# A hybrid decoder on one core: the PSUM bank of mLSTM's value sums

## The chip, the core and the metric

The kernel runs on one NeuronCore of a Trainium2 chip, as one launch. The metric is device time in microseconds (us) from start to end of an execution, the median of the executions taken. The engines are called PE (TensorE), ACT (ScalarE), DVE (VectorE), POOL (GpSimd) and SP (SyncE, which issues most DMAs). PSUM, where PE's results land, has eight banks.

## The reference

Two decoder layers work on 512 tokens of width 1024 in float32. Each layer projects the normalised input to four mixers of 256 columns each, sums their outputs through `w_out`, then adds cross attention on 256 memory rows and a gated feed-forward network. The four mixers are hgrn2 (a gated recurrence in chunks), DSA (an index branch picks 128 keys for each query, then attention on those), NSA (compressed, selected and window attention) and mLSTM. What matters here is mLSTM, head by head, and the two others that use the bank in question:

```python
# mLSTM, one chunk of one head
s   = einsum('td,sd->ts', q, k) * d_mat          # scores times decay
num = ... + einsum('ts,sv->tv', s, v)            # value sums
den = ... + sum(s, axis=-1)
h   = num / max(abs(den), exp(-m_t))
# DSA, index branch
rel   = relu(einsum('thd,sd->hts', iq, ik))
score = einsum('hts,th->ts', rel, iw);  idx = top_k(score, 128)
# NSA
o = gate0 * o_cmp + gate1 * o_slc + gate2 * o_swa
```

The kernel takes mLSTM over all 512 tokens at once instead of in chunks, and takes its denominators from a 65th column of ones beside the 64 value columns.

## The kernel before, in words

Matrix products keep float32 accuracy by splitting each operand into a high and a low part, so that most products are three matmuls (`mm_T`, lines 329 to 331 of the profile; `mm_tok`, lines 339 to 341). Weights come by DMA, are split by ACT and POOL (lines 292, 293), or come already split.

**Stages of a layer.** Stage one, inside the first `weave` of `run`, holds the input projections (`proj_T`, `proj_tok`), DSA's index branch and top-k (`dsa`), all of NSA (`nsa`, `nsa_cmp`) and all of mLSTM (`ml`). Stage two, the second `weave`, holds DSA's attention, hgrn2 (`hg`), the part of the output projection that needs NSA and mLSTM (`out_stage(0)`), the memory's keys and values (`xa_kv`) and `out_stage(1)`. Then come cross attention and the feed-forward network. In layer 0, stage one lies at about 25 to 273 us of the span and in layer 1 at about 850 to 1100 us.

**The order of work.** The parts are generators. `mix` always advances the one that is least far along, by the costs that they yield against totals in the table `COST`. That fixes one program order. The scheduler of the tile framework then takes program order as priority, sets every engine's own order by a simulated timeline, and puts in the waits. On the chip each engine runs its list in order.

**PSUM in stage one.** The tags and their banks: `acc` two (projections), `tp` one, `sc` two and `o` one (NSA's attention), `dt` one, `mb` one. A tag with one bank holds one tile at a time, and a tile gives up the bank when its last reader has run.

- `mb` is mLSTM's own: two row transposes (L493) and two column transposes (L992), then for each of four heads four score tiles (L1048; DVE multiplies each by the decay into `m_p0` to `m_p3`, L1056, which have one buffer each) and one tile of value sums (20 matmuls, L1065). DVE reads the sums twice: a copy of the denominators (L1069) and, after three small steps, the product into `mo` (a `tt` call, L351). The next head's first scores then get the bank.
- `dt` is shared by DSA's index branch (by the aliases of its pool: transposes of the queries L493 and, per block of queries, eight score tiles L679, each read by ACT at L681) and NSA's compressed branch (L1200, L1208, L1220, L1239, L1244, L1263). At NSA's end two tiles of it take the compressed values (L1161), each read by DVE into `mo`, which needs NSA's window and selected attention to be done.

Counting the yields of the generators gives the program order of the tiles on `dt`, in both layers: index block 1 (two transposes, eight scores); of index block 2 two transposes and one score; two tiles of the compressed branch (L1200, L1208); the other seven scores of block 2; the rest of the compressed branch up to L1263; block 3 (two transposes, eight scores); the two L1161 tiles. mLSTM's first score tile comes after all of these in program order, and then mLSTM's heads 0, 1, 2, 3, each with four score tiles and its sums. In time, mLSTM's heads run beside NSA's attention and index block 3.

mLSTM's convolutions for heads 2 and 3 (L1006 to L1016) write `m_hi0` and `m_hi1`, with one buffer each, which the scores of heads 0 and 1 read.

**Around the end of stage one.** The top-k of block 3 (`select`, L696 and L697) runs 16 rounds on DVE. The projection `hgi` writes `h_v` (L485), whose memory is that of the index branch. `out_stage(0)` transposes mLSTM's output (L1281 into `tp` of the second stage's banks) and multiplies it with `wo0` in eight groups on `acc`; behind these, on the same tag, come `xa_kv` and `out_stage(1)`.

Of the kernel before, what the change touches and what calls it, by code (L numbers as in the profile page):

```python
# [17 lines left out]
TB = S // 128  # L18
# [188 lines left out]
class Kernel:  # L207
# [760 lines left out]
    def ml(self, pool):  # L968
# [34 lines left out]
        def conv(c):  # L1003
            x = self.m_x[c]
            y = self.t2(pool, "m_y", [128, S])
            nc.scalar.activation(y, x[:, 0:S], AF.Identity, scale=self.col("conv_w", 4 * c), bias=self.col("conv_b", c))  # L1006
            for j in range(1, 4):
                nc.vector.scalar_tensor_tensor(y, x[:, j:j + S], self.col("conv_w", 4 * c + j), y, op0=OP.mult, op1=OP.add)
            th = self.t2(pool, "m_th", [128, S])
            nc.scalar.activation(th, y, AF.Tanh, scale=0.5)  # L1010
            z = th
            nc.vector.scalar_tensor_tensor(z, th, 1.0, y, op0=OP.add, op1=OP.mult)
            hi = self.t(pool, f"m_hi{c // 2}", [128, S], FR, bufs=1)
            lo = pool.tile([128, S], FR, name="m_lo", tag="m_x", bufs=4)
            nc.scalar.activation(hi, z, AF.Copy)
            self.tt(lo, z, hi.bitcast(FT), OP.subtract, nc.gpsimd)  # L1016
            return hi, lo
# [10 lines left out]
        for h in range(4):  # L1028
            po = 64 * (h % 2)
            if h % 2 == 0:  # L1030
                while h and self.m_have < 2:
                    yield 0.2
                q = conv(h // 2)
                yield 3.0
                k = conv(2 + h // 2)
                yield 3.0
            Mb = self.t(pool, "m_Mb", [128, S], bufs=2)
            nc.scalar.dma_start(Mb, bass.AP(tensor=dap.tensor, offset=dap.offset + h * S, ap=[[0, 128], [1, S]]))
            Md = self.t2(pool, "m_Md", [128, TB, 128])
            self.tt(Md, Mb.rearrange("p (t c) -> p t c", t=TB), self.k("mlm")[:, None, :].to_broadcast([128, TB, 128]),  # L1040
                    OP.add, nc.gpsimd)
            pT = []
            for sb in range(TB):
                n = S - sb * 128
                sc = self.psum("mb")
                r = slice(po, po + 64)
                for j, (kk, qq) in enumerate(((k[0], q[0]), (k[0], q[1]), (k[1], q[0]))):
                    nc.tensor.matmul(sc[:, :n], kk[r, sb * 128:sb * 128 + 128], qq[r, sb * 128:],  # L1048
                                     start=(j == 0), stop=(j == 2))
                d = self.t2(pool, "m_d", [128, S])  # L1050
                ac = a_col[:, sb, h:h + 1]
                nc.scalar.activation(d[:, 0:128], Md[:, sb], AF.Exp, bias=ac, scale=-1.0)
                if n > 128:
                    nc.scalar.activation(d[:, 128:n], Mb[:, sb * 128 + 128:], AF.Exp, bias=ac, scale=-1.0)
                p = self.t(pool, f"m_p{sb}", [128, n], bufs=1)
                nc.vector.scalar_tensor_tensor(p, sc[:, :n], 1.0 / 32, d[:, :n], op0=OP.mult, op1=OP.mult)  # L1056
                pT.append(p)
                yield 1.0
            while not self.m_have:
                yield 0.2  # L1060
            ps = self.psum("mb", (128, TB, 65))
            for tb in range(TB):
                for sb in range(tb + 1):
                    c = (tb - sb) * 128
                    nc.tensor.matmul(ps[:, tb], pT[sb][:, c:c + 128], self.m_v1[:, sb, h], start=(sb == 0), stop=(sb == tb))  # L1065
            hh = ho[:, :, h]
            den = self.t(pool, "m_den", [128, 4, TB])
            dc = ps[:, :, 64]
            nc.vector.tensor_copy(den[:, 0], dc)  # L1069
            nc.vector.scalar_tensor_tensor(den[:, 0], den[:, 0], -1.0, den[:, 0], op0=OP.mult, op1=OP.max)  # L1070
            self.tt(den[:, 0], den[:, 0], e_col[:, :, h], OP.max)
            nc.vector.reciprocal(den[:, 1], den[:, 0])
            self.tt(hh, ps[:, :, 0:64], den[:, 1, :, None].to_broadcast([128, TB, 64]), OP.mult)
            yield 1.0
            sq = self.t2(pool, "m_sq", [128, TB, 64])
            nc.scalar.activation(sq, hh, AF.Square)
            nc.vector.tensor_reduce(den[:, 2], sq, axis=AX.X, op=OP.add)
            self.rsqrt(pool, den[:, 3], den[:, 2], 4.0 / 64, 4 * EPS)
            self.tt(hh, hh, den[:, 3, :, None].to_broadcast([128, TB, 64]), OP.mult)
            self.tt(hh, hh, og4[:, :, h], OP.mult)  # L1080
            yield 1.0
# [549 lines left out]
```

## Time and profile before

| what | value |
|---|---|
| median of 3 runs | 1665.04 us (1662.25 to 1666.55) |
| the profiled execution's own time | 1668.55 us |
| its span | 1666.8 us |
| mean granted TensorE clock | 0.978 of full speed |
| PE busy | 1598.7 us, 96% of the span |
| DVE, ACT, POOL busy | 920.8, 711.5, 799.8 us |

The span goes from the first to the last instruction of the profiled execution; its time adds what lies around that. "Busy" is time in which the engine had an instruction in work, and the ends of pipelined matmuls are modelled. A granted clock of 1.00 is 2.4 GHz and 0.50 is 1.2 GHz.

### The profile page before, as it was taken

What the parts mean: (1) busy time and instruction counts of PE and PEld (TensorE: products, weight loads), DVE (VectorE), ACT (ScalarE), POOL (GpSimd) and SP (SyncE); (2) the same over time, 40 slices, a digit from 0 to 9 for tenths busy, and PEclk for the clock granted to TensorE, in tenths of its full rate; (3) what the DMA queues carried; (4) which work ended last, traced back from release to release, by engine and by line L of the source; (5) the groups of instructions that cost most, each with busy time, mean ns of one, the idle gap of its engine ahead of it and who ended that gap; (6) DMA issues with size and microseconds to landing.
All of it is one profiled execution on the core that took longest, in us unless ns stands there. A gap on an engine that the chain in (4) does not pass through costs nothing.

```text
span 1666.8 us, 25488 instructions
## 1 busy us (share of the span) xinstructions
PE 1598.7 (96%) x9262; PEld 1326.0 (80%) x9262; DVE 920.8 (55%) x1760; ACT 711.5 (43%) x1525; POOL 799.8 (48%) x698
## 2 busy tenths in 40 slices
PE   7899997999899989999999999999998999999999
PEld 7878876878788868888898887787877888888887
DVE  5697678976764330344225884779776544124420
ACT  5565453356654443343324443433665433223321
POOL 5664334566448987874412010145662444444442
PEclk9999997999999999999999999979999999999999
DMA  5342212213248999963355733131141233333331
GB/s 162 88 114 79 70 32 86 63 49 107 83 140 290 318 311 315 309 216 90 106 158 180 263 111 133 51 118 52 38 125 33 76 95 91 93 101 95 94 100 66
DMA packets 114365, 212.72 MB, mean 128 GB/s; under 512 B 12984, under 2 KB 30136, under 8 KB 114240
## 3 DMA queue, kind: packets, MB, share of 16 engines
q1 hardware_dynamic: 111888, 206.11, 39.8%
q10 hardware_dynamic: 2032, 3.94, 0.7%
q8 instruction: 73, 1.20, 0.3%
q0 software_dynamic: 320, 1.05, 0.2%
q14 instruction: 52, 0.43, 0.1%
HBM read 170.69 MB, written 40.35 MB: 127 GB/s over the span
## 4 chain that ended last, share of the span: by engine, by line
PE 82%; DVE 9%; issue 2%; DMA 2%; POOL 2%; ACT 2%; SPq 0%; ACTq 0%; POOLq 0%; DVEq 0%
PE acc L329 13%; PE acc L331 13%; PE acc L330 13%; PE sc L330 5%; PE sc L331 5%; PE sc L329 5%; PE acc L339 4%; PE acc L340 3%; PE acc L341 3%; PE hb L856 2%; PE o L574 2%; PE sc L552 2%; PE tp L493 2%; POOL wl L293 1%; PE mb L1048 1%
## 5 line engine op out<-in xcount | busy, mean ns | idle before, releaser
L293 POOL TENSOR_TENSOR wl<-wr,wh 128x512 fp32r<-128x512 f32 (+5 forms) x432 | 548.9, 1279 | 462.0 <-ACT wh L292 441.1
L292 ACT ACTIVATE wh<-wr 128x512 fp32r<-128x512 f32 (+5 forms) x432 | 252.4, 592 | 339.0 <-PE acc L330 137.1
L329 PE MATMUL acc<-xh,wh 128*128 128x512 f32 (+1 forms) x704 | 274.0, 391 | 1.6 <-DVE xT L466 0.7
L330 PE MATMUL acc<-xl,wh 128*128 128x512 f32 (+1 forms) x704 | 272.4, 387 | 0.0
L331 PE MATMUL acc<-xh,wl 128*128 128x512 f32 (+1 forms) x704 | 272.4, 387 | 0.0
L466 DVE TENSOR_TENSOR xT<-acc,xT 128x512 f32<-128x512 f32 (+1 forms) x112 | 67.8, 610 | 215.7 <-PE acc L331 215.5
L329 PEld LDWEIGHTS acc<-xh,wh 128*128 128x128 f32 x704 | 132.7, 189 | 32.5 <-issue 2.4
L331 PEld LDWEIGHTS acc<-xh,wl 128*128 128x128 f32 x704 | 132.5, 188 | 27.6 <-issue 0.4
L330 PEld LDWEIGHTS acc<-xl,wh 128*128 128x128 f32 x704 | 132.7, 189 | 26.4 <-issue 0.2
L329 PE MATMUL acc<-f_gh,wh 128*128 128x512 f32 x352 | 139.0, 397 | 6.7 <-ACT f_gh L1491 6.7
L339 PE MATMUL acc<-wh,xh 128*128 128x256 f32 (+2 forms) x480 | 140.1, 295 | 0.8 <-DMA wh<-whl 0.6
L330 PE MATMUL sc<-xl,wh 128*128 128x512 f32 x352 | 139.7, 397 | 0.0
L330 PE MATMUL acc<-f_gl,wh 128*128 128x512 f32 x352 | 139.3, 397 | 0.0
L331 PE MATMUL acc<-f_gh,wl 128*128 128x512 f32 x352 | 139.3, 397 | 0.0
L331 PE MATMUL sc<-xh,wl 128*128 128x512 f32 x352 | 138.8, 394 | 0.0
L340 PE MATMUL acc<-wl,xh 128*128 128x256 f32 (+2 forms) x480 | 138.4, 290 | 0.0
L329 PE MATMUL sc<-xh,wh 128*128 128x512 f32 x352 | 137.9, 393 | 0.0
L341 PE MATMUL acc<-wh,xl 128*128 128x256 f32 (+2 forms) x480 | 137.2, 288 | 0.0
L318 POOL TENSOR_TENSOR phl<-pr,phl 128x512 fp32r<-128x512 f32 (+3 forms) x72 | 94.7, 1316 | 37.4 <-ACT phl L317 30.9
L317 ACT ACTIVATE phl<-pr 128x512 fp32r<-128x512 f32 (+3 forms) x72 | 44.2, 613 | 137.6 <-DMA pr<-in_wst 127.8
L339 PEld LDWEIGHTS acc<-wh,xh 128*128 128x128 f32 x480 | 92.3, 193 | 5.1 <-issue 1.9
L340 PEld LDWEIGHTS acc<-wl,xh 128*128 128x128 f32 x480 | 92.8, 194 | 1.2 <-issue 0.5
(407 smaller groups left out, 3160.2 us busy)
## 6 DMA issues: line engine op xcount, KB each, us to landing
wr<-in_wst SPq DMA_DIRECT2D x332, 256.0 KB, 2.7
whl<-phl SPq DMA_DIRECT2D x52, 512.0 KB, 3.8
pr<-in_wst SPq DMA_DIRECT2D x52, 256.0 KB, 4.1
wh<-whl SPq DMA_DIRECT2D x52, 256.0 KB, 4.6
wl<-whl SPq DMA_DIRECT2D x52, 256.0 KB, 4.7
wr<-in_wst SPq DMA_DIRECT2D x48, 128.0 KB, 2.6
wr<-in_wst SPq DMA_DIRECT2D x32, 192.0 KB, 2.4
whl<-phl SPq DMA_DIRECT2D x8, 524.0 KB, 3.7
```

The costliest lines, as they stand in the source:

```text
L292: nc.scalar.activation(hi, raw, AF.Copy)
L293: nc.gpsimd.tensor_tensor(lo, raw, hi.bitcast(FT), op=OP.subtract)
L317: nc.scalar.activation(both[:, 0], raw, AF.Copy)
L318: nc.gpsimd.tensor_tensor(both[:, 1], raw, both[:, 0].bitcast(FT), op=OP.subtract)
L329: self.nc.tensor.matmul(acc, wh, xh, start=(j == 0), stop=False)
L330: self.nc.tensor.matmul(acc, wh, xl, start=False, stop=False)
L331: self.nc.tensor.matmul(acc, wl, xh, start=False, stop=(j == n - 1))
L339: self.nc.tensor.matmul(acc, xh[:, s], wh, start=(first and j == 0), stop=False)
L340: self.nc.tensor.matmul(acc, xh[:, s], wl, start=False, stop=False)
L341: self.nc.tensor.matmul(acc, xl[:, s], wh, start=False, stop=(last and j == n - 1))
L466: self.nc.vector.tensor_add(self.xT[c][:, cols], acc, self.xT[c][:, cols])
L493: self.nc.tensor.transpose(p[:rows, j * 128:j * 128 + 128], src(j), self.ident)
```

## The change

The tile of the value sums is asked for under the tag `dt` in place of `mb`; its shape, its matmuls and its readers stay as they are. The score tiles stay on `mb`. The number of banks stays as it is.

```diff
             while not self.m_have:
                 yield 0.2
-            ps = self.psum("mb", (128, TB, 65))
+            ps = self.psum("dt", (128, TB, 65))
             for tb in range(TB):
                 for sb in range(tb + 1):
```

## Rows read from the trace of the kernel before

**Rows 1.** The page: engines over the whole span, and the chain's shares by engine.
```profile
PE 1598.7 (96%) x9262; PEld 1326.0 (80%) x9262; DVE 920.8 (55%) x1760; ACT 711.5 (43%) x1525; POOL 799.8 (48%) x698
...
PE 82%; DVE 9%; issue 2%; DMA 2%; POOL 2%; ACT 2%; SPq 0%; ACTq 0%; POOLq 0%; DVEq 0%
```

**Rows 2.** Windows: stretch, length, busy us (instructions) per engine; granted clock, DMA share, GB/s.
```profile
178.00:240.00 62.00, 61.83 (x371) 47.77 (x370) 40.01 (x69) 32.92 (x73) 24.87 (x18) 1.00 0.23 64
240.00:273.00 33.00, 23.89 (x150) 17.46 (x150) 30.80 (x78) 9.16 (x24) 2.29 (x2) 0.77 0.26 84
273.00:300.00 27.00, 26.80 (x202) 25.47 (x200) 21.30 (x37) 12.81 (x27) 21.32 (x24) 0.90 0.21 58
300.00:345.00 45.00, 44.97 (x271) 35.53 (x272) 39.52 (x86) 15.36 (x42) 21.50 (x22) 1.00 0.18 51
...
1068.00:1096.00 28.00, 22.38 (x137) 17.13 (x136) 26.41 (x67) 8.35 (x20) 2.29 (x2) 0.78 0.26 88
```

**Rows 3.** Waits near stage one's end: PE and ACT, layer 0; PE and ACT, layer 1.
```profile
PE tp L1281 <- DVE mo L351: 4.1, 1, 4.1
...
ACT m_sq L1076 <- DVE mo L351: 13.0, 1, 13.0
...
PE mb L1048 <- DVE mo L351: 1.0, 1, 1.0
...
ACT m_sq L1076 <- DVE mo L351: 10.5, 2, 10.0
```

**Rows 4.** Timeline, layer 0: index block 2's operand, its scores, the compressed branch between.
```profile
83.27 0.57 ACT L497 ACTIVATE iqT<-dt 96x512 fp32r<-96x512 f32 x1
...
83.89 0.69 PE L679 MATMUL dt<-ikT,iqT 96*128 96x384 f32 x1 [2.08 <-ACT iqT L497]
...
103.14 0.34 PE L1200 MATMUL dt<-kc,n_hid 64*128 64x64 f32 x2
...
116.69 0.34 PE L679 MATMUL dt<-ikT,iqT 96*128 96x384 f32 x1
```

**Rows 5.** Timeline, DVE: the second L1161 tile read, layer 0 and layer 1.
```profile
260.68 0.69 DVE L351 TENSOR_TENSOR mo<-mo,dt 128x512 f32<-128x512 f32 x1
...
1086.61 0.68 DVE L351 TENSOR_TENSOR mo<-mo,dt 128x512 f32<-128x512 f32 x1
```

**Rows 6.** Timeline, layer 0: head 0's sums; head 3's first scores, sums and last read.
```profile
178.55 2.34 PE L1065 MATMUL mb<-m_v,m_p 128*128 128x65 f32 x20
...
254.45 0.49 PE L1048 MATMUL mb<-m_hi,m_hi 64*128 64x512 f32 x1
...
263.80 4.53 PE L1065 MATMUL mb<-m_v,m_p 128*128 128x65 f32 x20 [0.73 <-DVE m_p L1056]
...
271.90 0.41 DVE L351 TENSOR_TENSOR mo<-mb,m_den 128x256 f32<-128x256 f32 x1
```

**Rows 7.** Windows of one line: L1065 (two heads' sums), then L1048 (two heads' scores).
```profile
178.00:240.00 62.00, 4.91 (x40) 4.72 (x40) 1.00 0.23 64
...
990.00:1068.00 78.00, 6.17 (x24) 3.62 (x25) 1.00 0.29 99
```

**Rows 8.** Timeline, layer 0: `hgi`'s blocks leave `acc`, PE resumes; PE resumes in layer 1.
```profile
272.74 0.82 ACT L485 ACTIVATE h_v<-acc,r 128x256 f32<-128x256 f32 x2
...
273.25 0.58 PE L339 MATMUL acc<-wh,xh 128*128 128x256 f32 x1
...
1095.99 0.56 PE L339 MATMUL acc<-wh,xh 128*128 128x256 f32 x1
```

**Rows 9.** Timeline, layer 0: convolutions of heads 2 and 3, first and last step; second L1281.
```profile
218.41 0.74 DVE L1008 SCALAR_TENSOR_TENSOR m_y<-m_x,cols,m_y 128x512 f32<-128x512 f32 x1
...
231.66 0.63 ACT L1015 ACTIVATE m_hi<-m_th 128x512 fp32r<-128x512 f32 x1 [0.27 <-DVE m_th L1012]
...
302.78 0.60 PE L1281 MATMUL tp<-kc,mo 128*128 128x128 f32 x4
```

## The prediction

> **What bounds the kernel now.** The page first: PE is busy 1598.7 of 1666.8 us and 82% of the chain that ended last is PE, with DVE next at 9% [rows 1]. So all idle time of PE together is 68 us, and a change that adds no matmul can only move that idle time, or the clock. Then the windows around the place of the change, the second half of stage one and what follows [rows 2]. From 178 to 240 us PE is full (61.83 of 62.00). From 240 to 273 it is busy only 23.89 of 33.00 at a mean clock of 0.77, while DVE is busy 30.80: here DVE and the waits set the pace. From 273 on PE is full again (26.80 of 27.00, then 44.97 of 45.00). Layer 1 has the same hole (22.38 of 28.00 at 0.78). Third, the waits in that hole [rows 3]: PE stood 4.1 us before the first L1281, ACT 13.0 us before mLSTM's L1076, both for DVE's read of head 3's sums; in layer 1 ACT stood 10.5 us in two waits there, and PE 1.0 us for a score tile until the sums of the head before had been read. Last, the timeline of the tiles on `dt`, below.
>
> **What the change asks for.** On `mb` each head's first scores wait for the read of the sums before. With the sums on `dt` that wait goes. Its direct price is small: 1.0 us seen on PE in layer 1, and the L1281 wait of 4.1 us, which is a wait for the last read on a bank that the second stage takes over [rows 3]. No instruction is added or taken away.
>
> **Where the sums stand in the bank's row.** This decides the sum. The trace shows how `dt` is given out. Index block 2 had its transposed queries at 83.84 us (83.27 + 0.57) and its first score at 83.89; ACT read that at once, and yet the second score, with the same operands, came at 116.69. Between them lie the tiles of the compressed branch, which wasn't ready until 103.14 [rows 4]. The bank stood empty for some 18 us while a ready score waited: it goes round in program order, not to whoever is ready. Layer 1 repeats the pattern. mLSTM's sums come after the two L1161 tiles in program order. Those wait for NSA's end: the second was read by 261.37 us (260.68 + 0.69) in layer 0 and 1087.29 in layer 1 [rows 5]. Head 0's sums, at 178.55 now [rows 6], therefore start at about 261, or as much earlier as NSA ends earlier without mLSTM beside it (I allow up to 10 us). Heads 1 to 3 follow, since `m_p0` to `m_p3` have one buffer each and head 0's sums still have to read them. The scores of heads 1 to 3 keep `mb`, but only the first score of each head can be made ahead of its `m_p` buffer.
>
> The Trainium skill (PSUM — Partial Sum Buffer, Summary: rules for kernel authors) says that a bank that is read should not be the one that PE writes next, but a different one. By that rule the change is right, and it would save the waits just named and no more; the rows on `dt` speak against it here.
>
> **Term A, PE work that moves.** Two heads' sums take 4.91 us of PE and two heads' scores 6.17 at full clock [rows 7], so a head is 2.46 + 3.09 = 5.5 us. Now all four heads are done when PE becomes full again. After the change I expect head 0's sums and head 1's scores before that point, and head 1's sums and heads 2 and 3 behind it: 2.46 + 2 x 5.55 = 13.5 us of PE work. What they leave behind in 178 to 240 can't be filled: program order has no projection left that isn't held by `acc`, since `hgi`'s first two blocks sit in its two banks until 272.74 [rows 8]. Behind 273 PE is full, so the moved work adds its length. Bounds: 0 (all of it falls into later holes) and 22 us (four heads). Nearest rows: PE's windows behind 273, with 0.2 us idle in 72; I take 13.5.
>
> **Term B, an earlier restart.** PE resumed dense work at 273.25 and 1095.99 [rows 8], behind head 3's sums (263.80, 4.53 us at half clock) and, in layer 0, behind ACT's 13.0 us wait and PE's 4.1 us wait [rows 3, 6]. These orders go, since head 3 is then far behind. What stays is DVE's top-k, which fills DVE in that stretch (30.80 of 33.00 [rows 2]). Bounds of the gain: 0, and the 13.0 and 10.5 us that ACT stood. I take 6 us per layer: the 4.1 us wait plus some 2 us of mLSTM's DVE work that leaves the stretch.
>
> **Term C, behind it.** The chain of heads is now serial: from 261.4, head 0's sums 2.5, three heads of 13.9 (254.45 to 268.33 for head 3 [rows 6]), and the convolutions of heads 2 and 3, which wait for head 1's scores, 13.9 (218.41 to 232.29 [rows 9]); together 319 us, and some 4 us for the last read. The transposes of `mo` that `out_stage(0)` needs came at 302.78 [rows 9], so it may be 20 us late, or not at all if the heads run at PE's pace of 5.5 us. PE has hgrn2, DSA's attention and the moved 13.5 us to do meanwhile, which covers most of it. DVE was busy 39.52 of 45.00 from 300 on [rows 2], so hgrn2 gets a little later. Bounds 0 and 20 us; I take 3 us, nearer the lower end, because the moved work is the cover. If that cover fails, rival three is what is left.
>
> **Sum.** Per layer 13.5 - 6 + 3 = 10.5 us, for two layers 21 us. The profiled execution took 1668.55 us, 3.5 over the median of the runs, so the sum against its own time is 1689.6, and about 1686 beside the median.
>
> **The rivals.**
> *One, the bank goes to whoever is ready* (the change works as it reads). Head 0's sums at 178.55 would fall where `dt` is idle, and the later ones push the index scores by a few us at most. Gain: 4.1 + 1.0 us and about 1 us of small waits, 1659. Against it stand rows 4. Chance 0.10.
> *Two, the hole is filled.* The order holds, but with mLSTM out of the way ACT empties `hgi`'s blocks early and PE's projections run in the hole. Then B reaches its upper ends (23.5 us for both layers against 27 of A), and if PE keeps full clock there, a mean of 0.77 over 33 us and 0.78 over 28 us [rows 2] give back 7.6 + 6.2 us: 27 - 23.5 - 13.8 = -10, 1655. It decides once `h_v` leaves `acc` before about 262 us. Chance 0.12. Without the clock the two terms cancel to within 4 us: no change, 1668; chance 0.17.
> *Three, stage two starves.* The groups of `wo0` stand first on `acc`, and `xa_kv` and `out_stage(1)` queue behind them; if mLSTM ends near 323 instead of 272 us, PE has too little to do, and C is at its upper end: 13.5 - 6 + 20 = 27.5 per layer, 55 in all, 1720. It decides once mLSTM's last read is later than some 310 us in layer 0. Chance 0.20.
>
> **How the numbers follow.** My forecast has 0.41: 1686 us, by itself between 1673 and 1700. About 5 us (0.3%) is what a measurement of this kernel can tell from no change. Faster: 0.10 + 0.12 = 0.22. No change: 0.17. Slower: 0.41 + 0.20 = 0.61. The range runs from just under rival two's time to just under rival three's, 1653 to 1715; beyond it lie the far halves of these two, under 2 in 10.
>
> **What would show it.** Right: the first L1065 after the second read of an L1161 tile in both layers, four sets of sums close together behind some 255 us, `m_sq` no longer a 13 us wait of ACT, PE less than full before 240 and full at 265 to 300, and L1281 of mLSTM's output later than 302.78. The order of `dt` shows wrong if any L1065 stands before an index score of block 3. Term B is wrong if `h_v` still leaves at 272; term C if the next stage's PE windows show idle time of more than a few us. The forecast falls if the time is under 1670: then the moved work found a hole that I didn't see.

## The result, and the profile after

The changed kernel takes 1744.34 us (median of four runs, 1728.25 to 1762.37) beside 1665.8 us for the kernel before on the same chip: a ratio of 1.0435, 95% interval 1.0407 to 1.0464. It is slower by 78.5 us where the prediction said 21, and outside the range of 1653 to 1715. The ratio leaves out the slowest of the four executions, which counts as a slow one and is the one profiled, so that the trace shows a loss of 93.8 us of span (1760.6 against 1666.8).

The page of the changed kernel, engines over the span and the chain by engine:

```profile
PE 1667.0 (95%) x9257; PEld 1382.6 (79%) x9262; DVE 917.2 (52%) x1760; ACT 711.9 (40%) x1525; POOL 797.2 (45%) x698
...
PE 80%; DVE 10%; ACT 3%; issue 2%; DMA 2%; POOL 2%; SPq 0%; another core or an unknown queue 0%; ACTq 0%; POOLq 0%; DVEq 0%
```

The same matmuls as in [rows 1] keep PE busy 68.3 us longer, and PE's idle time grew from 68.1 to 93.6 us. More busy time with no more work goes with a lower clock: the mean granted clock is 0.931 where it was 0.978. On this page alone one would blame the clock. The experiments below look for what stands behind it.

The windows of the changed kernel, to be laid beside [rows 2], and then the last of these stretches in the kernel before (columns as there):

```profile
178.00:240.00 62.00, 59.92 (x389) 45.78 (x388) 28.05 (x57) 28.17 (x61) 16.67 (x12) 1.00 0.20 54
240.00:273.00 33.00, 22.13 (x99) 18.94 (x96) 21.50 (x56) 5.99 (x15) 1.43 (x2) 0.59 0.24 80
273.00:300.00 27.00, 25.32 (x138) 20.37 (x136) 15.86 (x17) 13.05 (x28) 17.46 (x13) 0.78 0.33 93
300.00:345.00 45.00, 41.76 (x188) 34.25 (x188) 31.86 (x67) 12.20 (x25) 20.50 (x25) 0.72 0.09 30
345.00:417.00 72.00, 70.47 (x476) 57.76 (x476) 54.53 (x121) 29.14 (x84) 31.73 (x40) 0.72 0.09 27
```

```profile
345.00:417.00 72.00, 70.18 (x564) 57.48 (x563) 51.52 (x103) 44.44 (x112) 48.34 (x53) 1.00 0.29 85
```

The column to read is the count. From 300 to 345 us PE starts 188 matmuls where it started 271, from 345 to 417 it starts 476 where it started 564, and yet it looks nearly as busy as before, at a clock of 0.72. The loss does not show as idle time of PE here. The Trainium skill (Perfetto Trace Analysis, Identifying the Most-Contended Engine) warns that the busy share of TensorE's matmuls is no good measure of how close a kernel is to the peak, since pipelined matmuls look smaller in the trace. These rows agree with the warning, though here the share looks too large.

The timeline of the changed kernel in layer 0 [rows 5, 6, 8]: the second L1161 product and its read, head 0's sums, head 1's second score, `h_v` leaving `acc`; then mLSTM's last read, its last square and stage two's first instructions.

```profile
243.51 2.03 PE L1161 MATMUL dt<-n_eT,n_vbd 128*128 128x512 f32 x2 [3.12 <-DVE mo L351]
...
245.57 0.69 DVE L351 TENSOR_TENSOR mo<-mo,dt 128x512 f32<-128x512 f32 x1
...
246.32 4.53 PE L1065 MATMUL dt<-m_v,m_p 128*128 128x65 f32 x20 [0.78 <-DVE mo L351]
257.80 0.68 PE L1048 MATMUL mb<-m_hi,m_hi 64*128 64x384 f32 x1 [6.95 <-DVE m_p L1056]
...
260.48 0.82 ACT L485 ACTIVATE h_v<-acc,r 128x256 f32<-128x256 f32 x2
...
314.53 0.42 DVE L351 TENSOR_TENSOR mo<-dt,m_den 128x256 f32<-128x256 f32 x1
...
315.04 0.42 ACT L1076 ACTIVATE m_sq<-mo 128x256 f32<-128x256 f32 x1 [6.86 <-DVE mo L351]
...
315.84 0.62 ACT L713 ACTIVATE ckvsq<-d_ckv 128x512 f32<-128x512 f32 x1
...
319.57 0.64 PE L716 MATMUL dt<-one,ckvsq 128*128 128x1 f32 x3
```

Head 0's sums wait for the read of the second L1161 tile, as predicted: 246.32 us instead of 178.55. mLSTM's last read comes at 314.53 instead of 271.90. Right behind it, in ACT's list and then in PE's, stands the start of stage two, DSA's attention (L713, L716). L716 in both layers gives the account of the loss; first the kernel before, then the changed one:

```profile
281.26 0.28 PE L716 MATMUL dt<-one,ckvsq 128*128 128x1 f32 x2
...
1103.94 0.28 PE L716 MATMUL dt<-one,ckvsq 128*128 128x1 f32 x2
```

```profile
319.57 1.71 PE L716 MATMUL dt<-one,ckvsq 128*128 128x1 f32 x8
...
1180.57 1.71 PE L716 MATMUL dt<-one,ckvsq 128*128 128x1 f32 x8
```

Stage two starts 38.3 us later in layer 0 and 76.6 us later in layer 1, twice 38.3. The other 17.2 us of the span's 93.8 lie behind L716 of layer 1. The trace of e1_head0 below has delays of the same size (L716 at 320.92 and 1187.47). So the question is why stage two starts late, and what part of that is the bank.

### The profile page after: what moved, and what is told of

It reads as the page before. It is cut to its first block, busy times and chain, and to the rows that moved or that the text cites. A ratio compares the mean times of both kernels' runs of the same rounds, so it can differ in the third digit from the quotient of the medians.

```text
span 1760.6 us, 25498 instructions
## 1 busy us (share of the span) xinstructions
PE 1667.0 (95%) x9257; PEld 1382.6 (79%) x9262; DVE 917.2 (52%) x1760; ACT 711.9 (40%) x1525; POOL 797.2 (45%) x698
## 4 chain that ended last, share of the span: by engine, by line
PE 80%; DVE 10%; ACT 3%; issue 2%; DMA 2%; POOL 2%; SPq 0%; another core or an unknown queue 0%; ACTq 0%; POOLq 0%; DVEq 0%
PE acc L329 13%; PE acc L330 12%; PE acc L331 12%; PE sc L330 5%; PE sc L331 4%; PE sc L329 4%; PE hb L856 4%; PE acc L339 3%; PE acc L340 3%; PE acc L341 3%; PE o L574 2%; PE sc L552 2%; PE tp L493 2%; PE mb L1048 1%; PE dt L1065 1%
## 5 line engine op out<-in xcount | busy, mean ns | idle before, releaser
L329 PE MATMUL acc<-xh,wh 128*128 128x512 f32 (+1 forms) x704 | 276.5, 395 | 5.9 <-ACT xh L1283 2.9
L331 PE MATMUL acc<-xh,wl 128*128 128x512 f32 (+1 forms) x704 | 275.1, 391 | 0.0
L329 PEld LDWEIGHTS acc<-xh,wh 128*128 128x128 f32 x704 | 133.9, 191 | 37.1 <-ACT xh L1283 3.7
L331 PEld LDWEIGHTS acc<-xh,wl 128*128 128x128 f32 x704 | 134.2, 191 | 27.2 <-POOL wl L293 0.4
L329 PE MATMUL acc<-f_gh,wh 128*128 128x512 f32 x352 | 138.9, 397 | 7.3 <-ACT f_gh L1491 7.3
L339 PE MATMUL acc<-wh,xh 128*128 128x256 f32 (+2 forms) x480 | 138.8, 292 | 1.3 <-ACT h_g L485 1.1
L331 PE MATMUL acc<-f_gh,wl 128*128 128x512 f32 x352 | 139.1, 396 | 0.0
L331 PE MATMUL sc<-xh,wl 128*128 128x512 f32 x352 | 138.8, 394 | 0.0
L329 PE MATMUL sc<-xh,wh 128*128 128x512 f32 x352 | 138.0, 393 | 0.0
L341 PE MATMUL acc<-wh,xl 128*128 128x256 f32 (+2 forms) x480 | 137.1, 287 | 0.0
L339 PEld LDWEIGHTS acc<-wh,xh 128*128 128x128 f32 x480 | 91.9, 192 | 4.1 <-ACT h_g L485 1.3
```

The lines of the kernel that those rows point to most:

```text
L329: self.nc.tensor.matmul(acc, wh, xh, start=(j == 0), stop=False)
L331: self.nc.tensor.matmul(acc, wl, xh, start=False, stop=(j == n - 1))
L339: self.nc.tensor.matmul(acc, xh[:, s], wh, start=(first and j == 0), stop=False)
L341: self.nc.tensor.matmul(acc, xl[:, s], wh, start=False, stop=(last and j == n - 1))
```

## The experiments

Theory at the start: the bank is given out in program order, so the sums wait for L1161, and mLSTM's end is late by what is left of that wait. Rivals: sharing the bank costs by itself; the half clock carries the loss; ACT's list carries it. What separated the costly kernels from the others in the end was none of these, but the place of stage two in the engines' lists, which the scheduler makes anew for every kernel. The column "place" in this table is where L716 of layer 0 stands in the list of instructions that the built program gives TensorE (an entry is a run of equal matmuls; e6_warm has 12 entries of its own products ahead of it). Times are medians in us, ratios against the kernel before on the same chip; the middle columns come from the timelines of layer 0.

| kernel | place | head 0's sums | last read | L716 | time | ratio (95%) |
|---|---|---|---|---|---|---|
| before | 1287 | 178.55 | 271.90 | 281.26 | 1665.8 | |
| after | 1397 | 246.32 | 314.53 | 319.57 | 1744.3 | 1.0435 (1.0407, 1.0464) |
| e1_head0 | 1397 | 246.21 | 315.36 | 320.92 | 1758.4 | 1.0555 (1.052, 1.059) |
| e2_head3 | 1300 | 178.29 | 270.13 | 280.86 | 1670.5 | 1.0034 (1.0022, 1.0045) |
| e3_head23 | 1400 | 177.37 | 293.11 | 300.89 | 1717.0 | 1.0333 (1.0271, 1.0394) |
| e4_cmp_o | 1398 | 233.61 | 306.20 | 311.05 | 1733.3 | 1.0398 (1.0361, 1.0435) |
| e5_early | 1398 | 219.99 | 301.84 | 306.05 | 1729.3 | 1.0384 (1.0367, 1.0401) |
| e6_warm | 1409 | 246.79 | 310.96 | 315.77 | 1756.2 | 1.0561 (1.0526, 1.0595) |
| e8_sqdve | 1396 | 246.57 | 308.11 | 313.02 | 1741.2 | 1.0442 (1.0392, 1.0492) |
| c8_sqdve | 1299 | 177.46 | 270.90 | 281.14 | 1670.0 | 1.0027 (1.0016, 1.0039) |
| e9_p2sq | 1397 | 249.17 | 296.83 | 304.33 | 1717.1 | 1.0306 (1.0279, 1.0333) |
| e9_sq | 1396 | 246.54 | 301.77 | 305.92 | 1739.0 | 1.0432 (1.0401, 1.0463) |
| c9_p2sq | 1239 | 179.16 | 269.53 | 270.96 | 1676.1 | 1.0053 (1.0033, 1.0073) |
| e11_head123 | 1397 | 175.80 | 301.61 | 306.65 | 1737.0 | 1.0428 (1.039, 1.0466) |
| c10_order | 1399 | 180.04 | 288.19 | 295.98 | 1716.4 | 1.0328 (1.0276, 1.038) |
| e12_all | 1286 | 233.44 | 272.24 | 277.94 | 1669.1 | 1.0032 (1.0019, 1.0045) |
| c11_early | 1286 | 175.96 | 274.82 | 281.19 | 1673.6 | 1.0059 (1.0044, 1.0074) |
| c12_sq | 1239 | 174.92 | 265.28 | 266.71 | 1668.5 | 1.0025 (1.001, 1.0039) |
| c13_sq_o | 1239 | 178.27 | 268.01 | 269.45 | 1669.9 | 1.0024 (1.0013, 1.0035) |

### Which heads: e1_head0, e2_head3, e3_head23, e11_head123

```diff
-            ps = self.psum("dt", (128, TB, 65))
+            ps = self.psum("dt" if h == 0 else "mb", (128, TB, 65))
```

This is e1_head0; in the order of the heading, the others have `h == 3`, `h > 1` and `h` as the condition.

> Only head 0's sums go to the index branch's bank; heads 1 to 3 keep mLSTM's own. Theory (the bank is given out in program order, so head 0's sums wait for NSA's second L1161 product, and the other heads wait for head 0 through mLSTM's score bank): nearly the whole loss, 1720 to 1750 us, with head 0's first L1065 at 240 to 250 us of layer 0 instead of 178.55. Rival (each head's sums on the shared bank cost about a quarter of the 78 us, whichever head it is): 1680 to 1690 us.

> Only head 3's sums go to the index branch's bank. Theory (program order): its sums ran at 263.80 us before, after the second L1161 read at 260.68 us, so nothing is made to wait: within 5 us of the kernel before, 1661 to 1671 us. Rival (a quarter of the loss for each head on the shared bank): 1680 to 1690 us.

> The sums of heads 2 and 3 go to the index branch's bank. Theory (program order): head 2's sums ran at 246.86 us before and now wait for the second L1161 read, some 0 to 14 us later in a layer: 1666 to 1690 us, near the lower end if L1161 itself comes earlier. Rival (a quarter of the loss for each head): 1695 to 1710 us.

> Heads 1 to 3 on the index branch's bank, head 0 on mLSTM's own. Theory (the first head sent there waits for L1161, and all behind it wait with it): head 0's sums stay at 178 us, head 1's go from 208.67 to 240 to 250 us; three heads then follow instead of four, 1720 to 1740 us, between the 1717 of heads 2 and 3 and the 1744 of all four. Rival (what counts is whether head 0 is sent there): within 15 us of the kernel before, 1665 to 1680 us.

Head 0 alone costs more than all four together (1758.4, 8 us above the range expected), head 3 alone next to nothing (1670.5): the rival of a quarter for each head is gone, and it matters where in the bank's row a head's sums stand. e11_head123 came as the theory had it (1737.0). e3_head23 did not: 1717.0 where 1666 to 1690 was expected, though head 2's sums came only 11 us later (257.68 instead of 246.86 us). Two thirds of the loss for 11 us of waiting was the first sign that the wait is not all.

### L1161 on another bank, mLSTM ahead in program order: e4_cmp_o, e5_early

```diff
-            o = self.psum("dt")
+            o = self.psum("o")
```

```diff
-COST = {"dsa": 74.0, "nsa": 140.0, "ml": 41.0, "in": 78.0, "mlin": 100.0, "two": 225.0, "attn": 49.42, "hg": 92.2, "out": 21.47, "ahead": 1834.58}
+COST = {"dsa": 74.0, "nsa": 140.0, "ml": 41.0, "in": 78.0, "mlin": 200.0, "two": 225.0, "attn": 49.42, "hg": 92.2, "out": 21.47, "ahead": 1834.58}
```

> The kernel after, with the two L1161 products on the bank of NSA's attention sums instead of the index branch's. Theory (program order): head 0's sums then wait only for the last scores of index block 3, read by 229 us, and start at 230 to 235 us of layer 0, some 13 us earlier than in the kernel after; in two layers, with the clock, 30 to 60 us of the 78 come back: 1685 to 1715 us. Rival (L1161 is not what they wait for, or mLSTM's later chain sets the end anyway): 1735 to 1750 us.

> The kernel after with mLSTM set ahead in program order (its stage cost 100 becomes 200): head 0's sums then ask for the bank before the last two scores of index block 3, head 1's before the L1161 products; heads 2 and 3 still stand behind them. Theory (the place in program order sets the wait): as with heads 2 and 3 alone, 1700 to 1725 us. Rival (the shared bank costs the same wherever its users stand): 1735 to 1765 us.

Both bring the sums forward, to 233.61 and 219.99 us, and both give back little, 11 and 15 us: 1733.3 and 1729.3 us lie between what the theory and the rival had expected, within neither. Head 0's sums are 26 us earlier in e5_early than in the changed kernel, mLSTM's last read 12.7 us.

### The half clock: e6_warm

```diff
                 r = slice(po, po + 64)
+                for j in range(4 if h else 0):
+                    nc.tensor.matmul(sc[:, :n], k[0][:, sb * 128:sb * 128 + 128], q[0][:, sb * 128:], start=True, stop=True)
```

> The kernel after with four products of 128 rows added ahead of the three of 64 rows in each score tile of heads 1 to 3 (48 a layer, overwritten by the real scores): TensorE gets more work in the stretch at half clock, and no new wait. At full clock they cost some 48 x 0.15 = 7 us a layer. Theory 1 (the half clock is an effect of the holes and holds up no chain): 1745 to 1775 us, since work is only added. Theory 2 (the half clock of 290 to 323 us is what makes mLSTM's last heads and the stage behind them late): the granted clock there goes to 1.00 and the time falls to 1700 to 1735 us.

The window of 290 to 310 us, first of the changed kernel, then with the added products:

```profile
290.00:310.00 20.00, 18.22 (x57) 13.55 (x56) 6.69 (x17) 6.02 (x16) 6.53 (x6) 0.50 0.26 73
```

```profile
290.00:310.00 20.00, 17.16 (x98) 12.99 (x98) 6.46 (x17) 6.46 (x17) 5.48 (x5) 1.00 0.21 60
```

The clock did go from 0.50 to 1.00 there, and 98 matmuls took less of PE than 57 had. mLSTM's last read came 3.6 us earlier (310.96 instead of 314.53), and the kernel took 11.9 us more, about the 14 us that two layers of added products were reckoned at. So the half clock between 290 and 310 us holds up next to nothing. The run settles nothing for the half clock behind L716: from there to the last L574 of layer 0 the mean clock is 0.90 here, but 0.88 in e1_head0, which has no added products, and 0.80 in the trace of the changed kernel.

### ACT's list: e8_sqdve, c8_sqdve

```diff
-            nc.scalar.activation(sq, hh, AF.Square)
+            self.tt(sq, hh, hh, OP.mult)
```

> The kernel after with the square of each head's output (L1076) on VectorE instead of ScalarE. In the kernel after, ScalarE stands 14.0, 9.5 and 6.9 us at that square for VectorE's mo, ahead of the convolutions of heads 2 and 3 and of the next stage's first instruction L713. Theory (the late sums hurt through ScalarE's queue, which is kept in order): L713 starts 10 to 20 us earlier in layer 0 than at 315.84 us, and 20 to 45 us of the loss come back: 1700 to 1725 us. Rival (the chain of scores, sums and their buffers sets mLSTM's end, and ScalarE only waits with it): 1738 to 1750 us.

> The kernel before with the same square on VectorE: its ScalarE stands 13.0 us (layer 0) and 10.5 us (layer 1) at it. Theory (ScalarE's queue holds up the start of the next stage): 5 to 10 us a layer come back, 1646 to 1658 us. Rival (it waits for what the next stage needs anyway): 1661 to 1670 us.

The wait itself, in the changed kernel from 240 to 345 us, is the largest of ACT:

```profile
ACT m_sq L1076 <- DVE mo L351: 30.4, 3, 14.0
```

Without it L713 starts 7.2 us earlier (308.65 us) and the time is the same within its interval (1741.2). On the kernel before it gains nothing either (1670.0). The longest wait of an engine was not on the path.

### The ties between the heads: e9_sq, e9_p2sq, c9_p2sq

```diff
-                p = self.t(pool, f"m_p{sb}", [128, n], bufs=1)
+                p = self.t(pool, f"m_p{sb}", [128, n], bufs=1 if sb == 3 else 2)
...
-            sq = self.t2(pool, "m_sq", [128, TB, 64])
+            sq = Mb[:, 0:256].rearrange("p (t d) -> p t d", t=TB)
...
-            pd = self.pool(index, "dsa", n2=4, n4=0, side="right")
+            pd = self.pool(index, "dsa", n2=2, n4=0, side="right")
```

> The kernel after with the two ties loosened by which a head waits for the sums of the head ahead of it: the weighted scores m_p of the first three blocks get two buffers, and the square of the output is written over m_Mb, which is done with, instead of into the ring that m_d goes round in (to make room, DSA's index ring has 2 buffers instead of 4). Theory (head by head, the late sums hold up the next head's scores through these buffers): head 1's scores run before 246 us, the sums of heads 0 and 1 both lie at 246 to 258 us, mLSTM's last read comes 15 to 30 us earlier than 314.53 us, and 25 to 50 us come back: 1690 to 1720 us. Rival (something else sets mLSTM's end, such as VectorE's selection of 240 to 270 us or TensorE's queue): 1735 to 1755 us.

> The kernel after with the square alone moved over m_Mb; m_p keeps one buffer, which still ties head 1's weighted scores to head 0's sums. Theory (both ties have to go): 1730 to 1750 us. Rival (the ring of m_d is the tie that counts): 1690 to 1725 us.

> The kernel before with the same two ties loosened (and the index ring of 2). Its sums share the bank of its scores, so that the next head's scores stay behind them whatever the buffers: theory, no change, 1660 to 1672 us. Rival (the ties cost time in the kernel before as well): 1645 to 1658 us, which would beat it. If the smaller index ring costs something by itself: above 1675 us.

e9_sq has the second edit alone, on the changed kernel; c9_p2sq has all three on the kernel before. The theory's numbers came out: loosening the tie of the square alone gives back nothing clear of the noise (1739.0), loosening both gives back 27 us (1717.1, last read at 296.83 us). The tie of `m_p` alone was not tried. The control shows that the three edits cost the kernel before 10 us (1676.1). Even so 51 us of loss remained with the heads freed of each other.

### The place in the lists: c10_order, e12_all, c11_early

Laid side by side, the lists fell into two kinds. Around L716 the kernel before and the changed kernel have:

```
1238 L1281 MATMUL tp<-kc,mo_106 128x128 x4
...
1287 L716 MATMUL dt<-one,ckvsq 128x1
```

```
1390 L1281 MATMUL tp<-kc,mo_106 128x128 x4
...
1396 L1281 MATMUL tp<-kc,mo_106 128x128 x4
1397 L716 MATMUL dt<-one,ckvsq 128x1 x4
```

Counted matmul by matmul, 96 of hgrn2's projections (L339 to L341, 128x256), 18 of the first `wo0` groups (L329 to L331) and 4 more of L1281 stand ahead of L716 in the changed kernel that stand behind it in the kernel before. Every kernel with L716 at 1396 to 1409 took 1716 us or more, every kernel with it at 1239 to 1300 took 1677 or less. What this does to mLSTM can be counted in the same lists: of the matmuls of L339 to L341 with 128x256, 240 stand ahead of the last of head 3's sums in the kernel before and in e12_all, 360 in c10_order and 384 in the changed kernel.

c10_order is the kernel before with the cost `"mlin"` of the table `COST` at 130 instead of 100, the same one-number edit as in e5_early. e12_all is the changed kernel with the edits of e4_cmp_o and e9_p2sq together. c11_early is the kernel before with 200.

> The kernel before, no bank changed: mLSTM's stage cost 100 becomes 130. In the queue that this gives TensorE, the next stage's first instructions (L1281, L716) come some 110 to 150 matmul groups later, behind HGRN's projections and the first wo0 products, as in the kernel after (L716 at place 1399 of the queue; 1287 before, 1397 after). Theory 1 (the loss is the place of the next stage in the fixed queues, which the late sums only bring about): 1700 to 1740 us though the bank is the old one. Theory 2 (the loss is the wait of mLSTM's sums for the shared bank): 1660 to 1675 us.

> The sums of all heads on the index branch's bank as in the kernel after, with L1161 on NSA's bank, two buffers for m_p and the square over m_Mb together (index ring of 2). In its TensorE queue L716 stands at place 1286, as in the kernel before. Theory 1 (the place of the next stage in the queues): nearly all of the loss back, 1670 to 1690 us. Theory 2 (the sums' wait for the bank): head 0's sums still start at 230 us or later instead of 178, and the time stays at 1700 to 1720 us.

> The kernel before with mLSTM's stage cost 200 (the control of the run in which the kernel after had it): bank unchanged, L716 at place 1286 of the queue. Theory 1 (place in the queue): 1655 to 1680 us. Theory 2 says the same, since no sums wait for the index branch. A time over 1700 us would fell both.

The two cross over. With the old bank and the new place, c10_order loses 53 us (1716.4). With the new bank and the old place, e12_all loses 5.7 us (1669.1), although head 0's sums start 55 us later than in the kernel before; its other edits also bring mLSTM's last read back to 272.24 us, so that it does not show what the wait costs without them. The timeline of c10_order, layer 0: head 0's sums, the last weighted score of head 3, the first and last of head 3's sums, DVE waiting for them, the last read, stage two.

```profile
180.04 2.12 PE L1065 MATMUL mb<-m_v,m_p 128*128 128x65 f32 x18
...
268.41 0.29 DVE L1056 SCALAR_TENSOR_TENSOR m_p<-mb,m_d 128x128 f32<-128x128 f32 x1 [1.06 <-PE mb L1048]
...
275.77 0.33 PE L1065 MATMUL mb<-m_v,m_p 128*128 128x65 f32 x2
...
285.82 0.78 PE L1065 MATMUL mb<-m_v,m_p 128*128 128x65 f32 x6
...
286.63 0.16 DVE L1069 COPY m_den<-mb 128x4 f32<-128x4 f32 x1 [17.93 <-PE mb L1065]
...
288.19 0.42 DVE L351 TENSOR_TENSOR mo<-mb,m_den 128x256 f32<-128x256 f32 x1
...
295.98 0.95 PE L716 MATMUL dt<-one,ckvsq 128*128 128x1 f32 x8
```

Head 3's 20 sums took 4.53 us in one piece in [rows 6]. Here they are strung out over 10.8 us among the projections, and DVE, which had made the last of their operands by 268.7 us, stands idle for 17.93 us until they are done. Nothing made PE do the projections first but its list. Then the window of 345 to 417 us, first of c10_order, then of e12_all:

```profile
345.00:417.00 72.00, 71.56 (x505) 60.02 (x508) 46.83 (x107) 35.62 (x96) 34.53 (x40) 0.72 0.08 23
```

```profile
345.00:417.00 72.00, 70.06 (x552) 57.17 (x554) 52.88 (x103) 45.98 (x118) 48.56 (x53) 1.00 0.29 89
```

c10_order has the sparse stage two of the changed kernel, at the same clock of 0.72, with the bank untouched; e12_all has the old one. The match is not full: in its profiled execution c10_order has L716 at 295.98 and 1143.00 us, 14.7 and 39.1 us late, two fifths and half of the changed kernel's delays, and the other 23 us of its loss of span lie behind L716 of layer 1. The control c11_early, at 1673.6, stays near the kernel before, so that a stage cost of 200 alone is not what e5_early lost by.

### Is there more in an earlier place: c12_sq, c13_sq_o

Both are the kernel before with the square over `m_Mb` (the diff stands above); c13_sq_o has L1161 on `o` as well.

> The kernel before with the square written over m_Mb and nothing else changed: in TensorE's queue the next stage's L716 comes at place 1239 instead of 1287. If an earlier place goes on paying beyond the old one: 1650 to 1661 us. If it is only a matter of before or behind the block of projections: 1662 to 1670 us. (The same with the index ring of 2 took 1676 us, so the smaller ring would have cost the difference.)

> The kernel before with the square over m_Mb and the L1161 products on NSA's bank, so that the index branch's bank is no longer asked for by NSA's end; sums on mLSTM's own bank as before; L716 at place 1239. If an earlier place pays further: 1650 to 1661 us. If not: 1662 to 1672 us.

L716 starts 14.6 and 11.8 us earlier than in the kernel before, and neither is faster (1668.5 and 1669.9). No version tried beats the kernel before.

## Why the prediction was wrong

**The order of the bank: right.** Head 0's sums start behind the second L1161 read in both layers, 15 us earlier than the 261 us of the text because NSA ends earlier; the text allowed 10. e1_head0 shows that this one wait is enough to bring the whole loss. Rival one is out.

**Term B: the event right, its worth not.** `h_v` left `acc` at 260.48 us, 12.3 us earlier than in [rows 8] and before the 262 us at which rival two was to decide. But the dense work that this let in stands ahead of the sums of heads 2 and 3 in PE's list: head 2's first scores started at 287.44 us, when the projections ahead of them had run and the convolutions had written `m_hi` (by 287.38 us). Rival two counted on a filled hole; from 240 to 273 us PE was busy 22.13 us at a clock of 0.59, where it had been busy 23.89 at 0.77.

**Term A: not tested as a sum.** mLSTM's PE work did move behind 246 us, but no more than that can be read off.

**Term C: the step that failed.** It took 3 us a layer, with 20 as the upper bound, because hgrn2 and DSA's attention were to cover mLSTM's late end: "which covers most of it". They did not. The projections that stood ahead in PE's list had run by 286 us, and the first instructions of DSA's attention and of hgrn2's recurrence stand behind mLSTM's last in the lists of ACT and PE and start when it ends (L713 at 315.84, L716 at 319.57, L836 at 320.31 us, behind a last read at 314.53). Measured at L716, a layer loses 38.3 us in the profiled execution. The bound of 20 was taken from 302.78, which is the second L1281 on mLSTM's output in layer 0; there is one before it. First the kernel before, then the changed one:

```profile
272.47 1.09 PE L1281 MATMUL tp<-kc,mo 128*128 128x128 f32 x4 [4.14 <-DVE mo L351]
```

```profile
313.48 1.06 PE L1281 MATMUL tp<-kc,mo 128*128 128x128 f32 x4
...
318.73 1.05 PE L1281 MATMUL tp<-kc,mo 128*128 128x128 f32 x4
```

The second came 16.0 us late (318.73 against 302.78), inside the bound, the first 41.0.

The text reckoned with the old lists, although the scheduler sets every engine's own order from a simulated timeline. A change that makes one part late in that timeline lets it plan the lists anew. c10_order shows that such a re-planning costs 53 us with the bank untouched, and e12_all that the new bank costs 5.7 us where the lists keep the old place, with L1161 moved and the ties loosened. How the 78.5 us of the changed kernel divide between its lists and the wait itself is argued from this, not shown: c10_order has the same matmuls ahead of L716 as the changed kernel, but in another order and with half of the delay at L716 of layer 1. The difference of some 25 us is about what e9_p2sq gave back by untying the heads with L716 at the same place.

**Rival three: the one that came.** Its mark, a last read later than some 310 us, was passed (314.53), and stage two did run with fewer matmuls (188 and 476 where there were 271 and 564). Its price, 27.5 us a layer or 1720 in all, was 11 us a layer short of the profiled 38.3, for the same reason as term C: its upper bound was the lateness of the second L1281 alone. The sign of the forecast held; rival three with 0.20 was given half the chance of the forecast with 0.41.

**The mark for term C misled.** "PE windows show idle time of more than a few us" was to fell it. Idle in 300 to 345 us is 3.2 us, about a few; the loss shows in the count of matmuls and the clock. Two marks of a right forecast did not come: ACT still stood 14.0 us before `m_sq` (30.4 in three waits), and the four sets of sums do not lie close together but from 246.32 to 313.68 us.

**What stays open:** which tie tips the scheduler from one kind of list into the other. e12_all without its L1161 edit is e9_p2sq, and without both loosened ties it is e4_cmp_o; both have the late place. Without one of the two ties it was not run, and nothing read from the trace of the kernel before says how near the tipping point is. Open too is what the low clock inside stage two costs, and what is cause and what is effect there.

## What to carry to other kernels

Where the order of each engine's work is planned from a simulated timeline, a change of a buffer can be a change of every list: compare the lists of the two kernels around the next stage's first instructions before costing waits. To price a bank shared by two branches, look for who is ahead in program order and what then ends last, not at the bank's idle time. And read a window's matmul count and granted clock together with its busy time, since PE looked 98% busy here with 476 matmuls at a clock of 0.72 as it had looked 97% busy with 564 at 1.00.

## What the runs showed of the hardware

- A stretch with mLSTM's 64-row scores and 65-column sums and some products of `wo0` ran at the half clock (0.50, or 1.2 GHz, over 290 to 310 us) with PE busy 18.22 of 20.00. PE had stood idle for 1.66 us up to 286.92 us, and the clock was at 0.50 from 288 us on. With four more 128-row products per score tile, it was 1.00 from 290 to 310 us. From 357 to 393 us the changed kernel stayed at 0.50 with PE shown as busy 36.00 of 36.00. I had not expected a PE that shows as busy to stay at 1.2 GHz for so long.
- Among kernels with the late place, the longest stages two are those with the lowest clock. The time from L716 to the last L574 of a layer, with 737 to 767 matmuls started in it, is 109.8 us at a mean clock of 0.90 (e6_warm, layer 0), 110.9 at 0.88 (e1_head0, layer 0), 121.8 at 0.77 (e9_sq, layer 1) and 130.6 at 0.71 (c10_order, layer 1). In layer 0 of the kernel before it is 113.1 us with 873 matmuls at 1.00. Whether the clock sets the length or follows from the thinner list is not shown.
